# Context rows transposed in one go, modulation columns between two products, one low split moved up, in a two-layer diffusion backbone

## The chip, the cores and the metric

The kernel runs on one core of a Trainium2 chip. The metric is the device time of one execution in microseconds (us); a version's time is the median of its runs. The profile is one execution of the same program, recorded by the hardware profiler.

## The reference

The reference is a small diffusion backbone with two layers, 512 latent tokens `x` and 256 context tokens `ctx`, each of width 1024. Layer 0 is a bidirectional retention mixer, layer 1 a gated spatial mixer (gMLP). Only the start of layer 0 matters here: every row is normalised, scaled and shifted by a vector that comes out of the conditioning `c` (for `x`) or `c_ctx` (for `ctx`), and then multiplied by a wide weight matrix.

```
shift_x, scale_x, gate_x = split(silu(c)     @ ada_w[0] + ada_b[0], 3)
shift_c, scale_c, gate_c = split(silu(c_ctx) @ ada_w[0] + ada_b[0], 3)
hx = rmsnorm(x, norm_g[0])   * (1 + scale_x) + shift_x
hc = rmsnorm(ctx, norm_g[0]) * (1 + scale_c) + shift_c
qx, kx, vx, zx = hx @ w_in;   qc, kc, vc, zc = hc @ w_in
```

`rmsnorm(x, g)` is `x * rsqrt(mean(x*x) + 1e-6) * g`.

## The kernel before

All data are float32. For accuracy each operand of a large product is split into a high part, rounded to the fast matmul type, and a low part, the rest; a product is then three matmuls (low by high, high by low, high by high). The high part is a cast on ScalarE (ACT), the low part a subtraction on VectorE (DVE). The program's names in the profile follow: `hl` is a split weight tile, `raw` the tile as it was loaded, `oA` and `oS` are split pieces of normalised `x`, `hc` is split normalised `ctx`, `xq` and `cq` are the loaded `x` and `ctx`, `pst` is any PSUM bank.

The activations lie transposed, features on the partitions, in K tiles of 128 features. `kb` counts the K tiles from 0 to 7. The first weights to be used are four tiles, B11, B12, B21 and B22: the first index is the half of the features (kb 0 to 3, kb 4 to 7), the second the output columns. `w11` and `w12` in the code are the first two while they are being split in pieces (`cut`, line 692; `Q.begin` gives the tile, `cut(tile, k0, k1)` casts K tiles k0 to k1 of it on ScalarE and returns the low split, which is run where it is called). `Q.upto(n)` splits whole weight tiles until n are done. The weights arrive from HBM through a stream that loads the next tile as soon as a slot is free.

The work at the start, for each K tile, is this:

- `ada0_mm` (line 553) multiplies the conditioning with the modulation weights of one or more K tiles. These are narrow matmuls, 32 columns wide, into a PSUM bank, which ScalarE copies out as `adae`.
- `ada0_cols` (line 569) turns `adae` into columns by transposes on TensorE (PE), and VectorE reduces them and makes the scale `gs` and the shift `sh` of that K tile.
- `come` (line 648) applies them to the rows of that K tile: a scaling on VectorE, the high part on ScalarE, the low part on VectorE.
- `plain` (line 673) multiplies the K tile with the weights. `plain(kb, th, nhs)` does the token half `th` (0 or 1 of `x`, 2 for `ctx`) for the weight tiles in `nhs`, six matmuls for each of the two.

Before `come` can run, the inverse root of each row's mean square is needed. `half_rows(src, g, t)` (line 520) transposes half of the features (`g`) of a block of 256 tokens (`t`; 2 is `ctx`) so that tokens stand on the partitions, in two groups of four transposes with a PSUM bank each; the first group's squares are summed by a Square on ScalarE, the second's by BATCH_NORM_STATS on VectorE. `inverse(t)` (line 531) makes the roots from the two halves, with a Sqrt on ScalarE between small operations on VectorE, and `spread(t)` (line 541) spreads them over the partitions by a product, whose result ScalarE copies to `rs`.

PSUM has eight banks: six for the tag "ps", of which four hold the running sums of the `x` products through this whole stage, and two for the tag "tm", which `ada0_mm`, `ada0_cols` and `spread` share. A tile takes a bank of its tag that is free, or waits until one is.

What is done in which order: TensorE goes in the order of the program text throughout (`pe.kept = True`). ScalarE and VectorE do the same from the first statistics until `hold("c")` behind the loop over kb = 2 to 7 (line 769):

```
    act.kept = dve.kept = True
    ...
    hold("c")
    Q.limit = PROJECTED
    act.kept = dve.kept = False
```

So in this stage an instruction that waits holds up everything behind it on its engine. Behind the loop the two are ordered by the program builder. The loads on SyncE's queue (SP) are issued in the order in which the builder puts them; each of the loads in flight has a semaphore of its own, and the next load is issued when one comes free.

All instructions appear at line 54 in the profile, the helper that records them, so the tiles' names and the times tell them apart.

Of the kernel before, what the change touches and what calls it, by code (L numbers as in the profile page):

```python
# [33 lines left out]
def f32(ap):  # L34
    return ap.bitcast(F32)
# [32 lines left out]
def hybrid_kernel(ctx, tc, xT_d, cT_d, cv_d, sv_d, rows_d, ada0_d, adag_d, w_d, rope_d, dec_d, ws_d, id_d, out_d):  # L68
# [3 lines left out]
    ps = ctx.enter_context(tc.tile_pool(name="ps", bufs=8, space=bass.MemoryType.PSUM))  # L72
# [9 lines left out]
    def st(shape, tag, dt=F32, bufs=1, name=None):  # L82
        return sb.tile(shape, dt, tag=tag, name=name or tag, bufs=bufs)
# [34 lines left out]
    def t2(name, shape=(P, 512), dt=F32):  # L118
        return st(list(shape), "t2", dt, bufs=T2, name=name)

    def pt(shape=(P, 512), tag="ps"):
        return ps.tile(list(shape), F32, tag=tag, name="pst", bufs=6 if tag == "ps" else 2)
# [222 lines left out]
    def features(bank, a, w, fresh, ks=range(4)):  # L345

        for kt in ks:
            if kt == 3 and inside:
                inside.pop(0)()
            r = (a[:, 0, kt, :], a[:, 1, kt, :])  # L350
            for s in range(2):
                o = s * 512 + kt * P
                mm3(bank[:, s * HS:s * HS + HS], (w[:, 0, o:o + P], w[:, 1, o:o + P]), r, fresh and kt == 0 and s == 0, kt == 3)
# [82 lines left out]
    cq = [st([P, 4, HS], f"g{2 + g}", name="cq") for g in range(2)]  # L436
# [80 lines left out]
    mvx = st([P, 3, 2], "mv", name="mvx")  # L517
    sq = [st([P, 2, 2], f"sq{t}", name="sq") for t in range(3)]

    def half_rows(src, g, t):  # L520

        for i in range(2):
            pq = pt()
            for k in range(4):
                pe.transpose(pq[:, k * P:k * P + P], src[:, k, i * P:i * P + P], ident)
            if i == 0:
                act.activation(t2("junk0"), pq, AF.Square, scale=1.0 / 32.0, accum_out=sq[t][:, g, 0:1])
            else:
                dve.bn_stats(bnx[:, t, g, :], pq)

    def inverse(t, then=None):
        s, mv = sq[t], mvx[:, t, :]
        dve.bn_aggr(mv, bnx[:, t, :, :])
        dve.scalar_tensor_tensor(s[:, 1, 1:2], mv[:, 0:1], mv[:, 0:1], mv[:, 1:2], ALU.mult, ALU.add)
        dve.tensor_tensor(s[:, 1, 0:1], s[:, 0, 0:1], s[:, 1, 0:1], ALU.add)
        act.activation(s[:, 1, :], s[:, 1, :], AF.Sqrt, bias=eps, scale=1.0)
        if then:
            then()
        dve.reciprocal(s[:, 1, :], s[:, 1, :])

    def spread(t):

        pr = pt((P, HS), tag="tm")
        for i in range(2):
            mm(pr[:, i * P:i * P + P], sq[t][:, 1, i:i + 1].to_broadcast([P, P]), ident, start=True, stop=True)
        return pr

    def copied(pr, name):
        rs = st([P, HS], name)
        act.copy(rs, pr)  # L550
        return rs

    def ada0_mm(*kbs, then=None):

        n = len(kbs)
        pa = pt((P, HS * n), tag="tm")
        for i, kb in enumerate(kbs):
            rows = ada_w.pop(kb)
            for k in range(KT):
                j = k % 4  # L560
                mm(pa[32 * j:32 * j + 32, i * HS:i * HS + HS], cpad[:, k, :], rows[k // 4][:, j * HS:j * HS + HS],
                   start=(k < 4 and i == 0), stop=(k >= 4), skip_group_check=True)
        if then:
            then()
        e = t2("adae", (P, HS * n))
        act.copy(e, pa)
        return e

    def ada0_cols(k0, e, n=1):
        pq = pt((P, HS * n), tag="tm")  # L570
        for b in range(2 * n):
            pe.transpose(pq[:, b * P:b * P + P], e[:, b * P:b * P + P], ident)
        s = st([P, 2 * n, 2], "ada_s" if n == 1 else "ada_s2", bufs=2, name="ada_s")
        v = pq.rearrange("p (c g r) -> p c r g", c=2 * n, g=4)
        dve.tensor_reduce(s, v[:, :, 0:2, :], axis=AX.X, op=ALU.add)
        ss = s.rearrange("p (n b) r -> p n b r", b=2)
        ks = slice(k0, k0 + n)
        dve.tensor_tensor(gs0[:, ks, :], ss[:, :, 0, :], adab0[:, 1, ks, :], ALU.add)
        dve.tensor_tensor(sh0[:, ks, :], ss[:, :, 1, :], adab0[:, 0, ks, :], ALU.add)
        dve.scalar_tensor_tensor(gs0[:, ks, :], gs0[:, ks, :], 1.0, g0[:, ks, :], ALU.add, ALU.mult)  # L580
# [67 lines left out]
    def come(*what, then=None):  # L648


        made = []
        for kb, th in what:
            g, k = divmod(kb, 4)
            r = th // 2
            if r:
                f, h, l = cq[g][:, k, :], hc[:, 0, kb, :], hc[:, 1, kb, :]
            else:
                name = NAMES[th][g]
                if k == 0:
                    A[name] = st([P, 2, 4, HS], AT_S3.get(name, "o" + name), F32R)  # L660
                f, h, l = xq[th, g][:, k, :], A[name][:, 0, k, :], A[name][:, 1, k, :]
            dve.scalar_tensor_tensor(f, f, gs0[:, kb, r:r + 1], rs[th], ALU.mult, ALU.mult)
            made.append((f, sh0[:, kb, r:r + 1], h, l))
        if then:
            then()
        for f, b, h, l in made:
            act.activation(h, f, AF.Identity, bias=b, scale=1.0)
        for f, b, h, l in made:
            dve.scalar_tensor_tensor(l, f, b, f32(h), ALU.add, ALU.subtract)
# [3 lines left out]
    def plain(kb, th, nhs=range(2), product=None):  # L673

        g = kb // 4
        for nh in nhs:
            if th == 0 and kb % 4 == 0:
                w0[g, nh] = Q.get(ahead=0)
        if th == 2:
            if kb == 0:  # L680
                bank["c"] = pt()
            features(bank["c"], hc[:, :, 4 * g:4 * g + 4, :], w0[g, 0], g == 0, (kb % 4,))
            return
        for nh in nhs:
            if kb == 0:
                bank[th, nh] = pt()
            if product:
                product(bank[th, nh], A[NAMES[th][g]], w0[g, nh], g == 0, kb % 4)
            else:
                features(bank[th, nh], A[NAMES[th][g]], w0[g, nh], g == 0, (kb % 4,))  # L690

    def cut(tile, k0, k1):

        hl, r, done = tile
        at = lambda x: x.rearrange("p (s k n) -> p s k n", s=2, k=4)[:, :, k0:k1, :]
        h, l = at(hl[:, 0, :]), at(hl[:, 1, :])

        def low():
            dve.tensor_tensor(l, at(r), f32(h), ALU.subtract)
            if k1 == 4:  # L700
                done()

        act.copy(h, at(r))
        return low
# [18 lines left out]
    rs[1] = copied(pr, "rs1")  # L723
    w12 = Q.begin()
    plain(0, 1, (0,), features_first)
    ada0_cols(1, es)
    cut(w12, 0, 1)()
    come((1, 0), (1, 1))
    plain(0, 0, (1,), features_first)
    plain(0, 1, (1,), features_first)  # L730
# [24 lines left out]
    def hold(*keys):  # L755

        for key in keys:
            i = len(held)
            if i % 2 == 0:
                two = st([P, 2, 512], f"g{1 + i // 2}", name="held")  # L760
            else:
                two = held[i - 1]
            held[i] = two
            act.copy(two[:, i % 2, :], bank[key])
            plain_done(key if key == "c" else f"{key[0] + 1}{key[1] + 1}", two[:, i % 2, :])
# [3 lines left out]
    for kb in range(2, 8):  # L769
        if kb == 3:  # L770
            Q.upto(3)
        plain(kb, 0)
        if kb in (2, 4, 6):
            ada0_cols(kb + 1, es, 1 if kb == 6 else 2)
        if kb + 1 < 8:
            come((kb + 1, 0), (kb + 1, 1))
        if kb == 4:
            half_rows(cq[1], 1, 2)
            inverse(2)
        if kb in (3, 7):  # L780
            Q.upto({3: 4, 7: 6}[kb])
        plain(kb, 1)
        if kb == 3:
            es = ada0_mm(5, 6)
            half_rows(cq[0], 0, 2)
        if kb == 4:
            es = ada0_mm(7)
        if kb == 2:
            Q.cap = None
            Q.pump()  # L790
        if kb == 4:
            rs[2] = copied(spread(2), "rs2")
        come(*((k, 2) for k in CTX_COME.get(kb, ())))
        if kb == 6:
            Q.upto(5)
        if kb == 7:
            hold((0, 0), (0, 1), (1, 0), (1, 1))
            op("S1")
            dve.tensor_tensor(f22, f21, f22, ALU.add)
            dve.tensor_tensor(shb, sh0[:, 0:4, 0], sh0[:, 4:8, 0], ALU.add)  # L800
            for k in range(4):
                shifted(f22[:, k, :], shb[:, k:k + 1], A["S1"][:, 0, k, :], A["S1"][:, 1, k, :])
        for k in CTX_PLAIN.get(kb, ()):
            plain(k, 2)
# [812 lines left out]
```

## Time and profile before

| | |
|---|---|
| median of 3 runs | 878.79 us (878.61 to 880.75) |
| profiled execution | 878.75 us |
| its span, first to last instruction | 876.7 us |
| TensorE matmul busy | 866.0 us, 99% of the span |
| VectorE busy | 712.2 us, 81% |
| ScalarE busy | 457.2 us, 52% |
| granted TensorE clock, mean | 0.998 |
| moved by DMA | 153.81 MB, mean 175 GB/s |

A row of the timeline gives the start in us from the span's start, the busy time in us, the engine, the line, the operation, `out<-in`, the size and the number of instructions that it merges; in brackets stands the idle time of the engine just before it and what ended that. PE is the matmul, PEld the weight load in front of each matmul, which overlaps with the matmul before; a row of PEld shows best when TensorE went on. A row of a tile of loads gives the issue's time and the time from issue to landing.

### The profile page before, as it was taken

Reading aid. Unit: us, or ns where it says so; the run is one execution under the profiler, and the core shown is the slowest. Engines: PE = TensorE matmul, PEld = TensorE weight load, DVE = VectorE, ACT = ScalarE, POOL = GpSimd, SP = SyncE. Lnnn points to the kernel's source line nnn. Section 1 sums busy time; section 2 is a strip of 40 time slices with the busy share of each in tenths; the row PEclk is TensorE's granted clock in tenths of the full one; section 3 lists DMA queues with packets and bytes.
Section 4 is the critical chain, followed back from the end, with each engine's and each line's share of the span. In section 5 each row is a group of like instructions: output and inputs, shape, how many; then the busy total and the mean of one; then the engine's idle time right before and its main releaser. Section 6 shows DMA issues by size and latency. Waiting matters only on the chain.

```text
span 876.7 us, 16965 instructions
## 1 busy us (share of the span) xinstructions
PE 866.0 (99%) x6890; PEld 826.8 (94%) x6890; DVE 712.2 (81%) x997; ACT 457.2 (52%) x707; POOL 58.3 (7%) x96
## 2 busy tenths in 40 slices
PE   8999999999999999999999999999999999999997
PEld 7799999999999999998989999999999899899986
DVE  4689978699789877878677688999899488688995
ACT  4465744444545435736255548844666546256434
POOL 0001211002101101000000001111000000000110
PEclk9999999999999999999999999999999999999999
DMA  9932967457677458848344511645435135035522
GB/s 349 405 129 97 303 239 267 150 174 241 193 237 243 145 165 328 286 127 272 132 156 158 165 52 70 200 153 196 142 133 180 36 121 192 25 121 168 121 44 102
DMA packets 75774, 153.81 MB, mean 175 GB/s; under 512 B 7728, under 2 KB 34864, under 8 KB 75696
## 3 DMA queue, kind: packets, MB, share of 16 engines
q1 hardware_dynamic: 67392, 128.40, 44.2%
q0 software_dynamic: 7872, 24.12, 8.2%
q8 instruction: 54, 0.88, 0.4%
q10 hardware_dynamic: 432, 0.20, 0.1%
q14 instruction: 24, 0.20, 0.1%
HBM read 128.58 MB, written 24.12 MB: 174 GB/s over the span
## 4 chain that ended last, share of the span: by engine, by line
PE 96%; DVE 1%; DMA 1%; ACT 1%; issue 0%; DVEq 0%; ACTq 0%
PE pst L54 96%; DMA raw<-in_w_dram 1%; DMA xq<-in_xT_dram 0%; DVE o L54 0%; ACT junk L54 0%; DVE xq L54 0%; DVE bnx L54 0%; DVE oA L54 0%; ACT oA L54 0%; ACT fss L54 0%; DVE gs L54 0%; DVE hl L54 0%; DVE sq L54 0%; ACT o L54 0%; DVE ada_s L54 0%
## 5 line engine op out<-in xcount | busy, mean ns | idle before, releaser
L54 DVE TENSOR_TENSOR hl<-raw,hl 128x1024 fp32r<-128x1024 f32 (+2 forms) x197 | 234.8, 1198 | 67.8 <-ACT hl L54 67.5
L54 ACT CAST hl<-raw 128x1024 fp32r<-128x1024 f32 (+2 forms) x197 | 202.8, 1033 | 137.1 <-DVE raw L54 59.3
L54 PE MATMUL pst<-oS,hl 128*128 128x256 f32 x1104 | 133.9, 279 | 0.1
L54 PE MATMUL pst<-hl,oS 128*128 128x256 f32 x1152 | 133.4, 276 | 0.0
L54 PEld LDWEIGHTS pst<-hl,oS 128*128 128x128 f32 x1152 | 131.8, 188 | 1.0 <-ACT snap L54 0.8
L54 PEld LDWEIGHTS pst<-oS,hl 128*128 128x128 f32 x1104 | 129.3, 188 | 1.6 <-PE pst L54 0.8
L54 PE MATMUL pst<-oA,hl 128*128 128x256 f32 x936 | 117.2, 280 | 1.7 <-DVE hl L54 1.2
L54 PEld LDWEIGHTS pst<-oA,hl 128*128 128x128 f32 x936 | 111.2, 188 | 4.5 <-DVE hl L54 1.6
L54 DVE TENSOR_TENSOR raw<-raw 128x1024 f32<-128x1024 f32 x92 | 111.9, 1218 | 0.8
L54 ACT COPY snap<-pst 128x512 f32<-128x512 f32 x92 | 53.6, 584 | 90.5 <-PE pst L54 90.3
L54 PE MATMUL pst<-hl,oA 128*128 128x256 f32 x768 | 91.6, 277 | 0.0
L54 PE MATMUL pst<-og,hl 128*128 128x256 f32 x768 | 91.1, 278 | 0.0
L54 PEld LDWEIGHTS pst<-og,hl 128*128 128x128 f32 x768 | 89.2, 188 | 0.3
L54 PEld LDWEIGHTS pst<-hl,oA 128*128 128x128 f32 x768 | 89.2, 188 | 0.1
L54 PE MATMUL pst<-v,ph 128*128 128x512 f32 x192 | 59.8, 393 | 0.0
L54 PE MATMUL pst<-hl,ya 128*128 128x512 f32 (+1 forms) x246 | 59.1, 386 | 0.0
L54 PEld LDWEIGHTS pst<-hl,ya 128*128 128x128 f32 x246 | 45.3, 188 | 9.5
L54 DVE TENSOR_TENSOR snap<-pst,snap 128x512 f32<-128x512 f32 x69 | 47.2, 684 | 6.2 <-PE pst L54 6.2
L54 PE MATMUL pst<-hl,hc 128*128 128x256 f32 x384 | 46.1, 276 | 0.0
L54 PEld LDWEIGHTS pst<-hl,hc 128*128 128x128 f32 x384 | 44.7, 188 | 0.0
L54 ACT CAST ph<-pf 128x512 fp32r<-128x512 f32 x24 | 14.8, 619 | 54.1 <-DVE pf L54 53.6
L54 PEld LDWEIGHTS pst<-v,ph 128*128 128x128 f32 x192 | 36.1, 188 | 7.3 <-issue 0.2
(181 smaller groups left out, 1022.3 us busy)
## 6 DMA issues: line engine op xcount, KB each, us to landing
raw<-in_w_dram SPq DMA_DIRECT2D x224, 256.0 KB, 4.1
bg<-in_adag_dram SPq DMA_DIRECT2D x32, 512.0 KB, 4.4
ada_w<-in_ada_dram SPq DMA_DIRECT2D x16, 512.0 KB, 9.1
raw<-in_w_dram SPq DMA_DIRECT2D x16, 512.0 KB, 4.3
bg<-in_dec_dram SPq DMA_DIRECT2D x12, 512.0 KB, 4.8
v<-snap POOLq DMA_DIRECT2D x16, 256.0 KB, 5.3
z<-snap POOLq DMA_DIRECT2D x16, 256.0 KB, 5.1
v<-v SPq DMA_DIRECT2D x8, 512.0 KB, 3.8
```

What stands on the lines that cost most here:

```text
L54: made = op(*args, **kw)
```

## The change

Three pieces of work are put elsewhere in the order of the text. None is added or taken out.

1. In the opening, the low split of the first K tile of `w12` stands before `ada0_cols(1, es)`, not behind it.
2. In the loop over kb, `plain(kb, 0)` is cut into its two weight tiles, and `ada0_cols`, where there is one (kb = 2, 4, 6), stands between them, not behind both.
3. The transposes of rows 512 to 1023 of the transposed ctx, that is features 512 to 1023 (`half_rows(cq[1], 1, 2)`), and the roots (`inverse(2)`) stand at the end of kb = 3, directly behind the transposes of the first half, and take their PSUM banks from the tag "tm". Before, they stood in kb = 4, between `come` and the second `plain`. The product that spreads the roots stays at the end of kb = 4.

```diff
-    def half_rows(src, g, t):
+    def half_rows(src, g, t, tag="ps"):
 
         for i in range(2):
-            pq = pt()
+            pq = pt(tag=tag)
...
     plain(0, 1, (0,), features_first)
+    cut(w12, 0, 1)()
     ada0_cols(1, es)
-    cut(w12, 0, 1)()
     come((1, 0), (1, 1))
...
     for kb in range(2, 8):
         if kb == 3:
             Q.upto(3)
-        plain(kb, 0)
+        plain(kb, 0, (0,))
         if kb in (2, 4, 6):
             ada0_cols(kb + 1, es, 1 if kb == 6 else 2)
+        plain(kb, 0, (1,))
         if kb + 1 < 8:
             come((kb + 1, 0), (kb + 1, 1))
-        if kb == 4:
-            half_rows(cq[1], 1, 2)
-            inverse(2)
         if kb in (3, 7):
             Q.upto({3: 4, 7: 6}[kb])
         plain(kb, 1)
         if kb == 3:
             es = ada0_mm(5, 6)
             half_rows(cq[0], 0, 2)
+            half_rows(cq[1], 1, 2, "tm")
+            inverse(2)
         if kb == 4:
             es = ada0_mm(7)
```

## The prediction

> **What bounds the kernel now.** I read the page first, then the chain that ended last in order of time, then the busy times by stretch, and last the timeline of the first 62 us, where every changed line lies.
>
> ```profile
> span 876.7 us, 16965 instructions
> PE 866.0 (99%) x6890; PEld 826.8 (94%) x6890; DVE 712.2 (81%) x997; ACT 457.2 (52%) x707; POOL 58.3 (7%) x96
> 44.08 65.93 PE pst L54 x576
> 60.00:110.00 50.00, 50.00 (x443) 50.00 (x442) 49.28 (x73) 32.60 (x45) 9.63 (x15) 1.00 0.56 183
> ```
>
> TensorE is the bound: it is busy in 99% of the span, and the chain is its own work in long unbroken pieces, one of them from 44.08 to 110. Before it TensorE stands still three times for longer: before 20.10, before 31.90 and before 44.08 (the rows follow, part by part). The changed lines lie at these three stops, and they are all that can be won here. The last row (from 60 to 110 us: stretch, PE, PEld, DVE, ACT, POOL, granted clock, DMA share, GB/s) shows that TensorE is never idle later, but also that VectorE has only 0.7 us to spare there.
>
> The profiled execution took 878.75 us, 2.05 more than its span, and the median shown is 878.79, so a gain read from the trace is taken off 878.75. A measurement of this kernel can tell about 0.3%, 2.64 us, from no change.
>
> **Part 1: low split of the second weight tile before the columns.**
>
> ```profile
> 18.46 0.41 ACT L54 CAST hl<-raw 128x256 fp32r<-128x256 f32 x1
> 18.92 0.30 PEld L54 LDWEIGHTS pst<-oA,hl 128*128 128x128 f32 x2
> 19.11 0.17 DVE L54 TENSOR_REDUCE ada_s<-pst 128x4 f32<-128x16 f32 x1 [0.82 <-PE pst L54]
> 19.62 0.42 DVE L54 TENSOR_TENSOR hl<-raw,hl 128x256 fp32r<-128x256 f32 x1
> 19.96 0.87 DVE L54 SCALAR_TENSOR_TENSOR xq<-xq,gs,rs 128x256 f32<-128x256 f32 x2
> 20.10 0.54 PEld L54 LDWEIGHTS pst<-oA,hl 128*128 128x128 f32 x4 [0.88 <-DVE hl L54]
> 21.45 0.59 PEld L54 LDWEIGHTS pst<-ada_w,cpad 128*32 128x32 f32 x16
> 22.45 0.77 PEld L54 LDWEIGHTS pst<-oA,hl 128*128 128x128 f32 x6 [0.41 <-issue]
> L54 SPq DMA_DIRECT2D ada_w<-in_ada_dram x1: 328/328/328, 12.3 to 12.3; - x1
> DMA to landing us min/median/max: 8.5/8.5/8.5
> ```
>
> The product can do two matmuls with the high half and then needs the low half, which VectorE makes at 19.62, behind four small operations on the modulation columns. Its input, the cast, is there at 18.87, and VectorE is idle until 19.11. Put first, the low half starts at 18.90, ends at 19.32, and TensorE goes on 0.06 later (20.04 to 20.10 now), at 19.38: **0.72 us**. Behind it the reduce starts 0.34 later than the low half (19.62 to 19.96 now), at 19.24, and the next row scaling 0.51 behind that, at 19.75 instead of 19.96, so the columns lose nothing that anyone waits for. What is late next: the modulation product moves from 21.45 to 20.73, and the second half of its weights lands at 12.3 + 8.5 = 20.8, but its ninth matmul is issued about a quarter of its 1.0 us (21.45 to 22.45) in, near 20.97. The 0.72 stands.
>
> **Part 2: columns between the two products of a K tile.**
>
> ```profile
> 27.52 1.48 PEld L54 LDWEIGHTS pst<-oA,hl 128*128 128x128 f32 x12 [0.41 <-issue]
> 27.66 0.59 ACT L54 COPY adae<-pst 128x512 f32<-128x512 f32 x1 [0.73 <-PE pst L54]
> 28.95 0.46 PEld L54 LDWEIGHTS pst<-ident,adae 128*128 128x128 f32 x4
> 29.68 0.19 DVE L54 TENSOR_REDUCE ada_s<-pst 128x8 f32<-128x32 f32 x1 [2.02 <-PE pst L54]
> 30.82 0.51 ACT L54 ACTIVATE oA<-xq,sh 128x256 fp32r<-128x256 f32 x1 [2.57 <-DVE xq L54]
> 31.36 0.48 DVE L54 SCALAR_TENSOR_TENSOR oA<-xq,sh,oA 128x256 fp32r<-128x256 f32 x1 [0.18 <-ACT oA L54]
> 31.38 0.19 PEld L54 LDWEIGHTS pst<-oA,hl 128*128 128x128 f32 x1 [0.56 <-ACT oA L54]
> 31.90 1.36 PEld L54 LDWEIGHTS pst<-oA,hl 128*128 128x128 f32 x11 [0.33 <-DVE oA L54]
> 51.31 0.17 DVE L54 TENSOR_REDUCE ada_s<-pst 128x4 f32<-128x16 f32 x1
> ```
>
> The loop runs for kb = 2 to 7; columns are made at 2, 4 and 6. At kb = 2 the chain from the transposes (28.95) over the reduce (29.68), ScalarE (30.82) and VectorE (31.36 to 31.84) ends the stop at 31.90. Twelve matmuls take 28.95 - 27.52 = 1.43, so six of them, 0.715, leave the path of the transposes. They could start at 27.52 + 0.715 = 28.24 in today's times, but their input is the ScalarE copy that ends at 28.25; with 0.03 to notice it (31.33 to 31.36 between the same two engines' rows), 28.28. The chain is 28.95 - 28.28 = **0.67 us** shorter. The six matmuls themselves are done behind the transposes, where TensorE would else wait 0.56 + 0.33. The stop is longer than what is taken from it, so the whole 0.67 counts; some 0.3 of it stays. At kb = 4 the same move only helps part 3. At kb = 6 the reduce at 51.31 shows no idle time in front of it: VectorE was the late one, and nothing is won or lost.
>
> **Part 3: rows 512 to 1023 of ctx and the roots in kb = 3.**
>
> ```profile
> L54 SPq DMA_DIRECT2D raw<-in_w_dram x1: 328/328/328, 27.0 to 27.0; - x1
> L54 SPq DMA_DIRECT2D cq<-in_cT_dram x1: 328/328/328, 28.3 to 28.3; - x1
> DMA to landing us min/median/max: 7.9/7.9/7.9
> 34.80 1.45 PEld L54 LDWEIGHTS pst<-ada_w,cpad 128*32 128x32 f32 x32
> 35.17 1.03 ACT L54 CAST hl<-raw 128x1024 fp32r<-128x1024 f32 x1
> 36.23 1.23 DVE L54 TENSOR_TENSOR hl<-raw,hl 128x1024 fp32r<-128x1024 f32 x1 [0.45 <-ACT hl L54]
> 36.67 0.86 PEld L54 LDWEIGHTS pst<-ident,cq 128*128 128x128 f32 x8 [0.41 <-issue]
> 36.81 0.58 ACT L54 COPY adae<-pst 128x512 f32<-128x512 f32 x1 [0.61 <-PE pst L54]
> 37.36 0.60 ACT L54 ACTIVATE junk<-pst 128x512 f32<-128x512 f32 x1
> 41.79 0.59 PEld L54 LDWEIGHTS pst<-ada_w,cpad 128*32 128x32 f32 x16
> 42.15 0.69 DVE L54 BATCH_NORM_STATS2 bnx<-pst 128x6 f32<-128x512 f32 x1
> 43.77 0.17 DVE L54 RECIPROCAL sq<-sq 128x2 f32<-128x2 f32 x1 [0.36 <-ACT sq L54]
> 44.05 0.52 PEld L54 LDWEIGHTS pst<-ident,sq 128*128 128x128 f32 x4 [1.67 <-issue]
> 44.49 2.82 PEld L54 LDWEIGHTS pst<-oA,hl 128*128 128x128 f32 x24
> ```
>
> Now the statistics of the second half start at 42.15, the root is ready at 43.94, and the product that spreads it waits until 44.05. The modulation product before it starts at 41.79 and takes 1.0 with its tail (part 1), so 1.26 of this is a stop. No instruction is added: eight transposes, one Square, one BATCH_NORM_STATS and six small ones stand earlier in their queues, and no DMA is moved.
>
> In the new order, with 0.72 + 0.67 = 1.39 taken off: the modulation product starts at 33.41, the first eight transposes at 35.28, the second eight could at 36.10. Their tile lands at 28.3 + 7.9 = 36.2: **0.10 lost**. ScalarE would reach the cast of the fourth weight tile at 35.17 - 1.39 = 33.78, but that tile lands at 27.0 + 7.9 = 34.9, so the cast runs from 34.97. That is the new wait. Behind it on ScalarE stand the copy of the modulation product, from 35.97, and the two Squares, from about 36.5 (0.55 behind the copy, as at 37.36 now) and 37.2 (0.7 for each with the read-out of its sum, an estimate from its 0.60); on VectorE the low half (36.03), two BATCH_NORM_STATS, the roots and only then the reduce of the columns. The second group of four new transposes shares two PSUM buffers ("tm") with that copy, which ends at 36.55; TensorE is there at 36.2 + 0.43 = 36.63 (half of the 0.86), so it does not wait. The eight end at 37.06, and the columns' transposes at kb = 4 come up at 37.06 + 0.715 = 37.77, and need the buffer that the second Square frees near 37.9: **0.14 lost**. The root then takes the 1.79 from 42.15 to 43.94, counted from about 37.8, and is ready near 39.6. The spreading product comes up only at 41.6. What is late next is the first half of kb = 5: its reduce stands behind the roots, near 39.55, and by the row distances of part 2 (29.68 to 31.84) its low half is ready near 41.7, against a product at 42.06: 0.3 to spare. So the stop of 1.26 goes and 0.24 comes: **1.02 us**. From the spreading product on, ScalarE, VectorE and TensorE all follow it, so the shift is handed on whole, and the long piece from 44.08 starts earlier by the sum.
>
> Sum: 0.72 + 0.67 + 1.02 = 2.41 us, 878.75 - 2.41 = **876.3 us**, 0.27% less. Not in the trace are the landings under the new order: as they stand they cost 0.24; 0.3 earlier they cost nothing, 0.5 later they cost about 0.5 more. I take them as they stand, since the queue is full in this stretch (413 to 418 GB/s below) and its order is unchanged. If all of the last two stops went (0.89 and 1.26, beside the 0.72), the gain would be 2.87; that is the ceiling.
>
> ```profile
> 27.50:31.00 3.50, 3.50 (x32) 3.29 (x28) 1.41 (x7) 0.77 (x2) 0.00 (x0) 1.00 1.04 418
> 31.00:34.80 3.80, 3.30 (x25) 2.96 (x24) 3.08 (x6) 2.11 (x5) 0.00 (x0) 1.00 1.03 413
> 41.80:44.50 2.70, 1.48 (x21) 0.86 (x21) 1.70 (x7) 1.04 (x4) 0.00 (x0) 1.00 1.09 368
> ```
>
> The Trainium skill, page "DMA: Bandwidth & Descriptors", section "Where 436 GB/s comes from", puts the ceiling of the ports at 435 GB/s and HBM's share of one core at about 358. The trace's 413 to 418 is past the second figure and 4% short of the first; at the ceiling both landings would come over 1 us earlier (an estimate) and the sum would be 2.65 instead of 2.41.
>
> **The rivals.** *A, the landings do not bite*, and perhaps what I leave of the stop in part 2 goes too: gain 2.65 to 2.87, 876.1 to 875.9. For it: a tile's landing needs only 0.3 us. Against: a full queue.
>
> *B, the roots' chain is late.* If the columns at kb = 4 get the PSUM buffer that the second half's BATCH_NORM_STATS frees, on VectorE behind a low half of 1.23, they wait until 38.5 instead of 37.9, and with landings 0.5 later they lose 1.1 in all: gain 1.3 to 1.8, 877.5 to 876.9. Against: ScalarE's part of the work is shorter by the rows above.
>
> *C, the clock falls.* The transposes and the narrow modulation product now stand in one piece of 33.41 to 37.06. If such work did not hold the clock, 3.5 us of full TensorE work (the row from 27.50) at half speed would cost 3.5: 879.8; two such pieces 883.3. It decides from 2.4 us lost. The Trainium skill, page "TensorE: Matmul & The Clock Gate", section "Part 4: PE-mode transpose", says that a transpose does not count as busy for the clock. Against it by the rows: the stretch with TensorE busy 1.48 of 2.70 us has a granted clock of 1.00, and so has every other.
>
> *D, slower by a changed order later on.* ScalarE and VectorE are held to the order of the text only up to the end of this loop; behind it the builder orders them by readiness. From 60 to 110 VectorE is busy 49.28 of 50. If one low split of 1.23 is put ahead of one that TensorE waits for, TensorE loses up to 1.23. Two such cancel the gain (878.8), five make 882.5. For it: the little room on VectorE. Against: all three engines are shifted alike, so nothing there becomes ready in another order.
>
> **How the numbers follow.** Forecast 0.52, with 2.1 to 2.9 us gained, 0.22 of it over 2.64; A 0.24; B 0.10; C 0.05, of which 0.03 beyond 0.3% slower; D 0.09, of which 0.08. Faster by over 0.3%: 0.22 + 0.24 = 0.46. Within: 0.30 + 0.10 + 0.02 + 0.01 = 0.43. Slower: 0.11. The range runs from A's far end, 875.9, to B's, 877.5, each with 0.4 to 0.5 for the spread of runs (the three shown differ by 0.2 and 2.1): 875.5 to 878.0. C and D are outside.
>
> **What would show it.** Right: TensorE goes on near 19.4 (part 1), starts kb = 3 near 30.5 (part 2), the reciprocal of the ctx roots ends near 39.6, the spreading product waits for nothing, and the long piece of the chain starts near 41.7. The cast of the fourth weight tile should sit behind a DMA, and the columns at kb = 4 behind a Square. Wrong: a wait of TensorE of over 0.5 us at kb = 4 or 5 (B), a granted clock under 1.00 before 50 us (C), new idle time of TensorE after 60 us (D).

## The result, and the profile after

The changed kernel takes 877.73 us in the median of 22 runs (876.75 to 879.20), the kernel before, run beside it, 878.79 (878.29 to 880.75). The ratio is 0.9984, with a 95% interval of 0.9978 to 0.9991: 1.4 us faster, between 0.8 and 1.9 (the two medians alone differ by 1.06). That lies inside the 0.3% that the prediction called no change, to which it gave a chance of 0.43 against 0.46 for more. It lies inside its range, but it is little more than half of the 2.41 us forecast.

The profiled execution of the kernel after took 879.01 us, with a span of 876.9, so it shows no gain at all. Its page, the lines of the span and of the busy times:

```profile
span 876.9 us, 16967 instructions
PE 868.4 (99%) x6890; PEld 829.7 (95%) x6890; DVE 713.0 (81%) x997; ACT 457.9 (52%) x707; POOL 58.4 (7%) x96
```

TensorE is busy 2.4 us longer than before (866.0) with the same 6890 matmuls. Two things make up most of that, and only one of them belongs to the change. The first is in the opening. The timeline of the kernel before, then that of the kernel after (start, busy time, engine, line, operation, tiles, count):

```profile
7.74 0.91 PEld L54 LDWEIGHTS pst<-ident,xq 128*128 128x128 f32 x8
16.64 0.59 PEld L54 LDWEIGHTS pst<-ada_w,cpad 128*32 128x32 f32 x16
25.66 0.81 PEld L54 LDWEIGHTS pst<-ada_w,cpad 128*32 128x32 f32 x20
```

```profile
8.75 1.66 PEld L54 LDWEIGHTS pst<-ident,xq 128*128 128x128 f32 x8
18.39 0.59 PEld L54 LDWEIGHTS pst<-ada_w,cpad 128*32 128x32 f32 x16
```

The same eight transposes take 0.91 in one execution and 1.66 in the other. No line of the change has run by then, yet everything in the trace of after is 1.75 us later when the modulation product of kb = 1 starts (18.39 against 16.64). It is TensorE's clock, which in this one execution became fast some 3.5 us later: in the traces' own record the full clock is granted from 6.80 us on before and from 10.28 on after. (The clock column of the view by stretch does not tell the two apart. It reads 1.00 from 7 to 10.2 us of after as well, where the transposes are slow, because the record begins only at 10.28.) So the two spans must not simply be subtracted. A second execution of the kernel after, below, has the early clock. Behind that start, the timeline of after reads:

```profile
20.51 0.42 DVE L54 TENSOR_TENSOR hl<-raw,hl 128x256 fp32r<-128x256 f32 x1 [0.47 <-ACT hl L54]
20.55 0.99 PEld L54 LDWEIGHTS pst<-oA,hl 128*128 128x128 f32 x6
22.38 0.59 PEld L54 LDWEIGHTS pst<-ada_w,cpad 128*32 128x32 f32 x16
29.19 0.42 PEld L54 LDWEIGHTS pst<-ident,adae 128*128 128x128 f32 x4
29.89 0.19 DVE L54 TENSOR_REDUCE ada_s<-pst 128x8 f32<-128x32 f32 x1 [1.35 <-PE pst L54]
32.11 1.32 PEld L54 LDWEIGHTS pst<-oA,hl 128*128 128x128 f32 x11 [0.23 <-DVE oA L54]
34.92 1.45 PEld L54 LDWEIGHTS pst<-ada_w,cpad 128*32 128x32 f32 x32
36.78 1.73 PEld L54 LDWEIGHTS pst<-ident,cq 128*128 128x128 f32 x16 [0.41 <-issue]
40.42 0.17 DVE L54 RECIPROCAL sq<-sq 128x2 f32<-128x2 f32 x1 [0.36 <-ACT sq L54]
41.88 0.59 PEld L54 LDWEIGHTS pst<-ada_w,cpad 128*32 128x32 f32 x16
42.88 0.52 PEld L54 LDWEIGHTS pst<-ident,sq 128*128 128x128 f32 x4 [0.41 <-DVE oA L54]
43.32 2.81 PEld L54 LDWEIGHTS pst<-oA,hl 128*128 128x128 f32 x24
```

All three edits do what they were to do. The six matmuls at 20.55 run through, where there was a stop of 0.88. Before kb = 3 a stop of 0.23 is left. The sixteen transposes of ctx stand in one piece at 36.78, and the first product of kb = 5 follows the modulation product of kb = 7 by 1.44 us (41.88 to 43.32), where it was 2.70 (41.79 to 44.49). From the modulation product of kb = 1 to the first product of kb = 5 the kernel after takes 24.93 us and the kernel before 27.85: 2.92 less, even more than the forecast ceiling of 2.87.

That gain is then partly given back. The stretch from 186 to 222 us, in the busy times by stretch, before and then after (the number in brackets counts the matmuls):

```profile
186.00:222.00 36.00, 36.00 (x320) 36.00 (x320) 33.77 (x39) 16.25 (x21) 5.04 (x8) 1.00 0.73 237
```

```profile
186.00:222.00 36.00, 36.00 (x308) 36.00 (x307) 32.94 (x37) 15.22 (x20) 5.06 (x8) 1.00 0.73 239
```

TensorE is busy all the time at a granted clock of 1.00 in both. But it gets 320 matmuls done before and 308 after: one each 112.5 ns, then each 116.9 ns. Two marks in the timeline, one product on each side of that stretch, before and then after:

```profile
157.11 2.89 PEld L54 LDWEIGHTS pst<-oA,hl 128*128 128x128 f32 x24
225.25 0.14 PEld L54 LDWEIGHTS pst<-ada_a,ones 128*32 128x32 f32 x4
```

```profile
155.94 2.89 PEld L54 LDWEIGHTS pst<-oA,hl 128*128 128x128 f32 x24
225.03 0.14 PEld L54 LDWEIGHTS pst<-ada_a,ones 128*32 128x32 f32 x4
```

The same matmuls on the same operands take 68.14 us before and 69.09 after: 0.95 us lost far behind the last changed line, with no wait to be seen.

### The profile page after: what moved, and what is told of

Same layout as the page of the kernel before. It is cut to its first block, busy times and chain, and to the rows that moved or that the text cites. A ratio compares the mean times of both kernels' runs of the same rounds, so it can differ in the third digit from the quotient of the medians.

```text
span 876.9 us, 16967 instructions
## 1 busy us (share of the span) xinstructions
PE 868.4 (99%) x6890; PEld 829.7 (95%) x6890; DVE 713.0 (81%) x997; ACT 457.9 (52%) x707; POOL 58.4 (7%) x96
## 4 chain that ended last, share of the span: by engine, by line
PE 97%; DVE 1%; DMA 1%; ACT 0%; issue 0%; ACTq 0%; DVEq 0%
PE pst L54 97%; DMA ident<-in_id_dram 1%; DVE o L54 0%; ACT junk L54 0%; DVE bnx L54 0%; DVE xq L54 0%; ACT fss L54 0%; DVE sq L54 0%; ACT o L54 0%; DVE fss L54 0%; ACT oS L54 0%; DVE oA L54 0%; ACTq L455 0%; DVE mvx L54 0%; DVE hl L54 0%
```

## The experiments

In all of them each kernel ran 11 times beside the kernel before, and the ratio is to those runs of the kernel before, not to the 878.79 of the first row. One table holds what they share. "kb 1-2" is the time from the start of the modulation product of kb = 1 to that of kb = 2, "2-3" on to that of kb = 3, "3-5" on to that of kb = 5, "5-7" on to that of kb = 7, and "7-P" on to the first product of kb = 5. "Stage" is their sum, and "marks" the time between the two marks just shown (157.11 to 225.25 in the kernel before). All are differences of two starts in the timeline of the profiled execution.

| kernel | median, us | ratio (95%) | kb 1-2 | 2-3 | 3-5 | 5-7 | 7-P | stage | marks |
|---|---|---|---|---|---|---|---|---|---|
| before | 878.79 | | 4.81 | 4.21 | 9.14 | 6.99 | 2.70 | 27.85 | 68.14 |
| after | 877.73 | 0.9984 (0.9978-0.9991) | 3.99 | 4.17 | 8.37 | 6.96 | 1.44 | 24.93 | 69.09 |
| e1 before, again | 879.37 | 1.0000 (0.9992-1.0009) | 4.81 | 4.21 | 9.06 | 6.98 | 2.70 | 27.76 | 68.14 |
| e2 after, again | 877.62 | 0.9983 (0.9974-0.9992) | 3.95 | 5.02 | 8.47 | 7.05 | 1.44 | 25.93 | 69.10 |
| e3 part 3 alone | 878.31 | 0.9997 (0.9988-1.0006) | 4.81 | 4.22 | 9.05 | 6.99 | 1.44 | 26.51 | 69.09 |
| e4 parts 1 and 2 | 878.01 | 0.9989 (0.9980-0.9998) | 3.95 | 4.44 | 8.39 | 7.19 | 2.10 | 26.07 | 68.14 |
| f1 part 1 alone | 878.47 | 0.9998 (0.9989-1.0007) | 3.95 | 4.66 | 9.06 | 6.98 | 2.69 | 27.34 | 68.14 |
| f2 no landing at kb = 2 | 877.77 | 0.9984 (0.9975-0.9993) | 3.98 | 4.19 | 9.02 | 7.21 | 1.45 | 25.85 | 69.10 |
| f3 two more warm-ups | 877.77 | 0.9988 (0.9979-0.9997) | 3.95 | 4.64 | 8.39 | 7.15 | 1.45 | 25.58 | 69.10 |
| f4 old PSUM tag | 879.24 | 1.0005 (0.9996-1.0013) | 3.95 | 4.99 | 8.39 | 8.43 | 1.44 | 27.20 | 69.10 |
| g1 after, slots back | 877.94 | 0.9986 (0.9977-0.9995) | 3.95 | 4.54 | 8.38 | 7.39 | 1.44 | 25.70 | 69.09 |
| g2 before, slots changed | 878.98 | 1.0000 (0.9991-1.0009) | 4.80 | 4.21 | 9.05 | 6.99 | 2.69 | 27.74 | 68.14 |
| g3 g1 with two more warm-ups | 877.76 | 0.9988 (0.9979-0.9996) | 5.06 | 4.22 | 8.38 | 6.96 | 1.44 | 26.06 | 69.09 |
| h1 one more wait | 877.48 | 0.9983 (0.9974-0.9992) | 3.95 | 4.21 | 8.81 | 7.53 | 1.44 | 25.94 | 69.09 |

### Both kernels again, and the parts alone

e1 and e2 are the two kernels unchanged; e3 takes only the third edit, e4 the first two, f1 the first.

```diff
# e3
-            pq = pt()
+            pq = pt(tag=tag)
...
-        if kb == 4:
-            half_rows(cq[1], 1, 2)
-            inverse(2)
...
             half_rows(cq[0], 0, 2)
+            half_rows(cq[1], 1, 2, "tm")
+            inverse(2)
# e4 (f1: the first two lines only)
+    cut(w12, 0, 1)()
     ada0_cols(1, es)
-    cut(w12, 0, 1)()
...
-        plain(kb, 0)
+        plain(kb, 0, (0,))
...
+        plain(kb, 0, (1,))
```

> The kernel before once more, unchanged, to see how far two profiles of one program differ. Stage time means from the weight load of the kb = 1 modulation product to that of the first product of kb = 5: 27.85 us in the profile before, 24.93 in the profile after. Theory A (the stage keeps its gain, the rest is chance: the moment at which TensorE's fast clock begins, and stretches in which the same matmuls come 118 instead of 113 ns apart): stage time 27.7 to 28.0, but the start of the fast clock and the matmuls at the slower spacing (1074 in the profile before) differ between the two profiles by hundreds. Theory B (the change lengthens those stretches and so gives gain back): again about 1074 of them, and the same total.

> The changed kernel once more, unchanged. Both theories: stage time 24.9 where the fast clock begins late, up to 25.4 where it begins early, since then two landings are met. Theory A: number of matmuls at the slower spacing other than 1376, by chance, and a gain in the median of 1 to 2.6 us. Theory B: 1376 within 100, and a gain of 1.0 to 1.6 us.

> Only the ctx rows and the roots are moved, with their PSUM banks from the other tag; the two other edits are undone. By the rows of before the stop of 1.26 us goes and no landing is met, since TensorE comes 1.4 later than with all three: stage time 26.6 (27.85 less 1.26), time 1.2 to 1.3 under before. If the landings or the shared banks were what costs, it would stay over 27.0.

> Only the low split and the columns are moved; the ctx rows and roots are where they were. By the prediction's first two terms 0.72 + 0.67: stage time 26.4 to 26.5, time 1.4 under before, and the stop in front of the spreading product stays at 1.2 to 1.3. If the third stop grew by what the first two lose, because something fixed in time ends it, stage time would stay at 27.8.

> Only the low split of the second weight tile is moved. The prediction gave it 0.72 us and 0.15 us to spare before the second half of the modulation weights of kb = 2 lands. In the repeated profiles that half landed at 20.92 to 21.92, not at 20.83. Theory A (this landing takes back part of the term): the weight load of that product's second half waits for the DMA by 0.3 to 1.1 us, and the time from the product of kb = 1 to the first product of kb = 2 (16.64 to 22.45, 5.81, in the profile before; 4.99 without a landing) is 5.2 to 5.8. Rival (the split itself gains less, because VectorE is late): no DMA wait there, and TensorE still idle behind a VectorE split. Time 0.1 to 0.7 under before.

e1 and e2 bear out a part of each theory. In the two traces of the kernel before, 1044 and 1236 weight loads start 116 to 119 ns behind the one in front of them; in the two of the kernel after it is 1324 and 1169 (the 1074 and 1376 of the expectations are by another count). So the total moves by 192 and by 155 from one execution of the same program to the next, as theory A has it, but the time between the marks does not move, as theory B has it. The stage of e3 came out as expected. That of e4 is 0.3 to 0.4 shorter than expected, since a part of the third stop went with the first two edits. f1 met the wait that its theory A expected, 0.77 us.

The timeline of e2, with the early clock:

```profile
18.48 0.97 PEld L54 LDWEIGHTS pst<-oA,hl 128*128 128x128 f32 x6
20.27 0.16 PEld L54 LDWEIGHTS pst<-ada_w,cpad 128*32 128x32 f32 x8
21.51 0.16 PEld L54 LDWEIGHTS pst<-ada_w,cpad 128*32 128x32 f32 x8 [1.08 <-DMA ada_w<-in_ada_dram]
33.76 1.45 PEld L54 LDWEIGHTS pst<-ada_w,cpad 128*32 128x32 f32 x32
35.29 1.05 ACT L54 CAST hl<-raw 128x1024 fp32r<-128x1024 f32 x1 [1.07 <-DMA raw<-in_w_dram]
38.12 0.46 PEld L54 LDWEIGHTS pst<-ident,adae 128*128 128x128 f32 x4
39.74 0.17 DVE L54 RECIPROCAL sq<-sq 128x2 f32<-128x2 f32 x1 [0.36 <-ACT sq L54]
40.81 0.59 PEld L54 LDWEIGHTS pst<-ada_w,cpad 128*32 128x32 f32 x16
41.81 0.52 PEld L54 LDWEIGHTS pst<-ident,sq 128*128 128x128 f32 x4 [0.41 <-issue]
42.25 2.36 PEld L54 LDWEIGHTS pst<-oA,hl 128*128 128x128 f32 x20
```

The third row is the point: the ninth matmul of the modulation product of kb = 2 waits 1.08 us for the second half of its weights. In the table it is the column "2-3": 5.02 against 4.21. e4 and f1 show the same wait, shorter. In the trace of after, which started 1.75 us later, the weights were there (they landed at 21.15, the product begins at 22.38, and "2-3" is 4.17). That makes 0.85 of the microsecond by which its stage is shorter than that of e2. The weights do not come later because TensorE comes earlier: their landing, issue and time to landing added, is at 20.83 in the trace of before, at 21.92 and 21.34 in e1 and e3, which do not have the first edit, and at 21.47, 20.92 and 21.01 in e2, e4 and f1, which do. By these figures the landings do not follow TensorE's time.

Column by column the parts are then clear. Part 1 takes 0.82 to 0.86 off "kb 1-2" in all kernels that have it but g3, and loses between nothing (h1, where the weights landed at 19.93) and 0.8 of it at the landing in "2-3". In g3 nothing is won: "kb 1-2" is 5.06 against 4.81. There the low split came first as well, but its input, the cast, waited for the weight tile itself:

```profile
19.16 0.40 ACT L54 CAST hl<-raw 128x256 fp32r<-128x256 f32 x1 [1.01 <-DMA raw<-in_w_dram]
```

That tile lands at 17.22 to 18.38 us in the other thirteen traces (18.38 in that of before) and at 19.08 in g3. Part 2 takes 0.67 off "3-5" in e2 (8.47 against the 9.14 of before) and up to 0.77 in the others that have it without a new landing. The other four traces without part 2 show 9.05 or 9.06; against them it is 0.58 or 0.59 in e2 and 0.66 to 0.69 in the others. Part 3 takes 1.26 off "7-P" in every kernel that has it. In e4, which keeps the second half of ctx at kb = 4, 0.6 of that stop goes as well, and 0.2 is paid in "5-7".

The times agree only roughly with this. e3 gains 1.3 us in the stage and shows no gain at all in its ratio; f1's 0.5 is not to be told from nothing; e4's 1.8 appear as 1.0 (0.2 to 1.8). The last column says why for e3 and e2: with part 3 the time between the marks is 0.95 longer than in all kernels without it. For e2 that leaves 1.9 - 0.95 = 0.95 us, and its ratio says 1.5 (0.7 to 2.3). By the same working e4, which loses nothing between the marks, should beat e2 by 0.8. In the traces it does, by 0.7 (spans of 874.6 and 875.3 us), but in the medians it does not. The execution of e4 that was profiled took 876.70 us. It and one of 876.71 are the fastest of the eleven, and the other nine took 877.61 to 878.70. Whether those nine had another spacing is not on record, since only one execution of each kernel was profiled. So the 0.95 is shown for the profiled executions, and not for all.

### Is the landing at kb = 2 what keeps the gain down?

f2 reads the first half of the weights of kb = 2 twice, so that the modulation of that K tile is another one and the second half need not have landed.

```diff
-  cpad[:, k, :], rows[k // 4][:, j * HS:j * HS + HS],
+  cpad[:, k, :], rows[0 if kb == 2 else k // 4][:, j * HS:j * HS + HS],
```

> All three edits, but the modulation product of kb = 2 reads the first half of its weights twice, so that it does not need the second half, which is still loaded; the modulation of that K tile is therefore another one. Theory A: without the wait of 1.08 us on this landing the stage takes 25.0 to 25.4 us (25.93 with it, where the fast clock began as early), the cast of the fourth weight tile and the ctx tile still wait for their landings, and the median is 0.5 to 0.9 us under the changed kernel's 877.6. Rival (the landing is hidden, since the later landings are met anyway): stage 25.8 to 26.0 and the same time as the changed kernel.

The wait of "2-3" is gone (4.19), but the stage is 25.85 against 25.93 and the median the same, as the rival has it. The reason stands in the timeline of f2:

```profile
24.62 1.02 PEld L54 LDWEIGHTS pst<-ada_w,cpad 128*32 128x32 f32 x24
26.47 0.16 PEld L54 LDWEIGHTS pst<-ada_w,cpad 128*32 128x32 f32 x8 [0.82 <-DMA ada_w<-in_ada_dram]
```

Now the product of kb = 3 and 4 waits, for the next load in the same queue. "3-5" is 9.02 where it is 8.4 in the others. A landing removed uncovers the next one. h1 shows the same without any such edit: there the weights of kb = 2 happened to land early, "2-3" is 4.21, and the next load is met:

```profile
26.15 0.16 PEld L54 LDWEIGHTS pst<-ada_w,cpad 128*32 128x32 f32 x8 [0.63 <-DMA ada_w<-in_ada_dram]
```

So in the early part of this opening TensorE can be moved earlier only by what the landings leave.

### Two more warm-up matmuls

```diff
-N_WARM = 10
+N_WARM = 12
```

> All three edits, with 12 in place of 10 filling matmuls in the opening. They fill the 0.5 to 0.65 us in which TensorE waits for the first transposes. Theory A on the clock (the fast clock begins at the end of a fixed interval in which TensorE was busy enough; the pause in front of the transposes sometimes makes it miss one, and then the opening takes 1.8 us longer): the late begin, at 10 us, no longer comes, the slowest runs are less than 1.5 us above the fastest (2.4 for the changed kernel over 22 runs), the median falls by 0.1 to 0.5. Rival (the begin of the clock is pure chance): the spread stays at 2 us or more. If the two matmuls delay the transposes instead: 0.2 to 0.4 slower.

The median does not move (877.77). The 11 runs of f3 lie within 0.9 us (877.29 to 878.21), where the 22 of the kernel after span 2.45. That shows nothing of the warm-up, though: with 10 filling matmuls the 11 runs of e1, f2, g1 and g2 lie within 0.84 to 1.10 us as well, and the full clock begins at 6.21 us in the trace of f3, later than in seven of the twelve traces with 10. Whether two more would prevent the late start stays open.

### Is the other PSUM tag needed?

```diff
-            half_rows(cq[1], 1, 2, "tm")
+            half_rows(cq[1], 1, 2)
```

> All three edits, but the second half of the ctx rows takes its PSUM banks from the tag of the first half, which has two free. By the changed kernel's rows its first four transposes wait for the Square of the first half (ends near 37.3 in the repeated profile) and the next four for its BATCH_NORM_STATS (near 38.2), where with the other tag they start at 36.5 and 37.0: stage 0.9 to 1.3 us longer than 25.93 with an early clock, time 0.6 to 1.3 us over the changed kernel. If banks do not matter: the same stage.

The timeline of f4:

```profile
36.08 0.85 PEld L54 LDWEIGHTS pst<-ident,cq 128*128 128x128 f32 x8 [0.41 <-issue]
38.05 0.42 PEld L54 LDWEIGHTS pst<-ident,cq 128*128 128x128 f32 x4 [1.12 <-ACT junk L54]
38.85 0.42 PEld L54 LDWEIGHTS pst<-ident,cq 128*128 128x128 f32 x4 [0.38 <-DVE bnx L54]
```

With four of the six "ps" banks held by the running sums, the second half waits for the Square (1.12) and for BATCH_NORM_STATS (0.38) of the first. "5-7" grows to 8.43, 1.38 over e2, and the kernel takes 879.24 us. The tag is worth 1.3 us in the stage (27.20 against 25.93), as expected, and 1.5 in the median, a little more than the 0.6 to 1.3 expected.

### What spaces the matmuls out behind the loop?

Without an exception, the nine kernels in the table that have part 3 take 69.09 or 69.10 us between the marks and the five without it 68.14. The matmuls between, their operands' places and their PSUM banks are the same in both sorts by the program, and so, between e3 and the kernel before, is the order of the instructions of ScalarE and VectorE behind the loop. I looked for something that part 3 moves as a side effect. The first find was a pair of the 2 KB tiles (`t2`): the tiles of the second Square and of the fifth and sixth modulation product become free in the other order, and two of the 11 slots change places in everything that follows. g1 turns that back in the kernel after, g2 does it in the kernel before, each by one small GpSimd copy that keeps the other tile in use longer; g3 is g1 with N_WARM 12.

```diff
# g1 (and g3)
+                junk[t, g] = t2("junk0")
-                act.activation(t2("junk0"), pq, AF.Square, ...
+                act.activation(junk[t, g], pq, AF.Square, ...
...
             rs[2] = copied(spread(2), "rs2")
+            nc.gpsimd.tensor_copy(junk[2, 1][:, 0:1], rs[2][:, 0:1])
# g2
-            es = ada0_mm(5, 6)
+            es = es56 = ada0_mm(5, 6)
...
             rs[2] = copied(spread(2), "rs2")
+            nc.gpsimd.tensor_copy(es56[:, 0:1], rs[2][:, 0:1])
```

> The kernel after, with one small instruction more: GpSimd copies one column into the junk tile of the second ctx Square, behind the copy of the spread roots at kb=4. It keeps that junk tile in use longer than the tile of the fifth and sixth modulation products, so that the small tiles of 512 columns (11 slots) are given out in the order of the kernel before: slots 7 and 9 change places in all that follows the loop. Theory (the microsecond given back behind the loop comes with the two slots): the stretch of matmuls at 118 ns from about 182 to 224 us is gone and the short one at about 157 to 184 us is back, the time from the first product of kb=5 to the end is 832.2 to 833.0 us instead of 833.0 to 833.8, and the median is about 876.7, 1.0 under the kernel after (ratio about 0.997). Rival (the stretch comes with the earlier start or with the order in which the roots of ctx are made, wherever the small tiles lie): the stretch at 182 to 224 us stays, 833.0 to 833.8 and a median of 877.7 (ratio 0.998).

> The kernel before, with the same small GpSimd instruction, but into the tile of the fifth and sixth modulation products: nothing of the change is made, only slots 7 and 9 of the small tiles change places behind the loop, as in the kernel after. Theory (slots): the stretch of matmuls at 118 ns from about 182 to 224 us appears, the time from the first product of kb=5 to the end is 833.0 to 833.8 instead of 832.2 to 833.0, and the median is about 880.0, 1.0 over the kernel before (ratio about 1.001). Rival (earlier start or order of the roots): no difference from the kernel before, 832.2 to 833.0 and a median of 878.9 to 879.1.

> The kernel after with the small GpSimd instruction of the run before last (slots as in the kernel before) and with N_WARM 12 instead of 10, which narrowed the spread of its runs. Theory (slots): as that run, time from the first product of kb=5 to the end 832.2 to 833.0, median about 876.7, with a spread of about 1 us over its runs. Rival: 833.0 to 833.8, median 877.8.

Busy times by stretch, g1 and then g2:

```profile
186.00:222.00 36.00, 36.00 (x308) 36.00 (x308) 32.91 (x38) 15.07 (x19) 5.05 (x8) 1.00 0.72 233
```

```profile
186.00:222.00 36.00, 36.00 (x320) 36.00 (x320) 33.69 (x38) 16.01 (x21) 5.05 (x8) 1.00 0.75 236
```

The theory falls, on both sides: with the slots of the kernel before, g1 still gets only 308 matmuls done, and g2, with those of the kernel after, 320. g3 is as g1. The second find was TensorE's own program: part 3 needs one instruction less that only waits (71 instead of 72), so all that follows stands one place earlier in the stream. h1 adds such a wait early in the loop, by a second identity tile:

```diff
+    ident2 = st([P, P], "rs2", name="ident2")
+    nc.gpsimd.tensor_copy(ident2, ident)
...
-  e[:, b * P:b * P + P], ident)
+  e[:, b * P:b * P + P], ident2 if k0 == 3 else ident)
```

> The kernel after, with a copy of the identity tile (made by GpSimd at the start) for the transposes of the modulation columns at kb=2. These then wait for two engines instead of one, and TensorE's program has one more instruction that only waits: 72 of them, as in the kernel before, where the kernel after has 71. Everything behind the loop then stands at the same number in TensorE's program as in the kernel before. Theory (the spacing of the matmuls behind a stop depends on where they stand in TensorE's stream of instructions): the stretch at 118 ns from about 182 to 224 us is gone and that of about 157 to 184 us is back, the time from the first product of kb=5 to the end is 832.2 to 833.0 us, with the stretch at 549 to 572 us deciding between the two, and the median is about 876.7 (ratio about 0.997), 1.0 below the kernel after. Rival (it comes with the earlier start or with the roots made at kb=3): the stretch at 182 to 224 us stays, 833.0 to 833.8, median 877.7. Both expect the start of the loop as in the kernel after, within 0.3 us.

```profile
186.00:222.00 36.00, 36.00 (x308) 36.00 (x307) 32.91 (x38) 15.06 (x19) 5.05 (x8) 1.00 0.73 238
```

308 again: this falls too. What is left is what the timeline shows of where the spacing turns, before and then e2:

```profile
167.27 1.83 PEld L54 LDWEIGHTS pst<-oS,hl 128*128 128x128 f32 x15
184.22 1.91 PEld L54 LDWEIGHTS pst<-hl,oA 128*128 128x128 f32 x16
```

```profile
165.06 2.80 PEld L54 LDWEIGHTS pst<-oS,hl 128*128 128x128 f32 x24
181.39 2.89 PEld L54 LDWEIGHTS pst<-hl,oA 128*128 128x128 f32 x24
```

Between these two rows lie 144 matmuls: 16.95 us before (117.7 ns each), 16.33 in e2 (113.4). Behind the second row it is the other way round (the 320 and 308 of the stretch). The two kernels leave a short stop for transposes, just ahead of the first row, with different spacing, and both change to the other spacing where the weight tile passes from the moving to the stationary operand. Read so, the spacing is a state that TensorE keeps, that turns over at stops and changes of operands, and that in the kernels with part 3 is the other way round from one such stop on. That is a reading of these rows and not tested by itself. Since the second stretch is more than twice as long as the first, the kernel before has the better side of it. Which property of part 3 does it stays open. The slots, the place in the stream and the order of the other engines behind the loop are excluded by g1, g2, h1 and e3. So is the tag: f4 has the old one and still takes 69.10. So is an earlier start alone: e4, without part 3, starts the first product of kb = 5 at 42.39 us and takes 68.14, while f4, with it, starts it later, at 44.08.

No version that was run is faster than the kernel after by more than the intervals. The one with the least in its trace is e4 (876.70 us in its profiled execution, the lowest of its 11 runs), but its median is 878.01.

## Why the prediction was right, and where not

**What bounds the kernel:** right. The gain and the losses are all TensorE's, and the opening is the only place where a wait was taken away.

**Part 1:** the term was nearly right (0.82 to 0.86 in "kb 1-2", forecast 0.72), but it stood on a landing that the working does not name: the cast at 18.46 came 0.08 behind the landing of its tile at 18.38. That tile mostly landed earlier, which made the term larger, and in g3 it landed at 19.08 and took the whole term. The sentence behind the term was wrong. "The 0.72 stands" rested on 0.15 us between a landing at 20.8 and the ninth matmul at 20.97, both from one execution. Over the fourteen traces the landing comes at 19.93 to 22.04, and the start of the stage lies at 16.18 to 16.88 where the clock was early. In e2 0.81 was lost there. A margin of 0.15 was no margin; it should have been a term with a range. It is rival A turned round: the landings bit in a place where the forecast had none.

**Part 2:** right in size (0.67 forecast; 0.58 to 0.77 measured, depending on the trace without part 2 that it is set against) and in what stays of the stop: 0.23 in the row at 32.11, some 0.3 forecast.

**Part 3:** right. The stop of 1.26 went whole. The cast of the fourth weight tile waits for a DMA, as forecast, until 35.29 (34.97 forecast, the landing 0.3 later). The reciprocal starts at 39.74 and ends at 39.91 (39.6), the spreading product comes up at 41.81 with nothing to wait for (41.6). The wait of 0.14 for the second Square is not in e2: the ctx tile landed at 36.47, TensorE came late enough, and the columns' transposes follow their matmuls at 38.12. In all "5-7" lost 0.06 instead of 0.24, and up to 0.54 in h1, where TensorE reached kb = 5 earlier against the same landing of the ctx tile (36.49).

**The sum:** 2.41 was forecast with the landings as they stood; e2 has 1.9, and the trace of after, for which the landings came in time, 2.92. The ceiling of 2.87 was a good figure for a kernel without landings. The two spans of before and e2 differ by 1.40 (876.7 and 875.3): 0.32 less before the stage, which is not the change's, 1.92 less in the stage, 0.02 more up to the first mark, 0.96 more between the marks, and 0.14 less behind them.

**"From the spreading product on the shift is handed on whole":** this is the step that failed. It holds as far as the first mark: from the first product of kb = 5 to it take 112.62 us before (44.49 to 157.11) and 112.64 in e2 (42.25 to 154.89). VectorE, with 0.7 us to spare, did no harm there. (In h1 it is 113.11; 0.23 of the excess is a stop of TensorE before 100.39, the only one between 60 us and the first mark that the timelines of the fourteen traces show.) Then 0.95 is lost to the spacing, for which the sum had no term. The argument looked at waits and at order, and a slower repetition of the same instruction is neither.

**The rivals:** A holds only in an execution that starts late. B did not happen. C did not: the sixteen transposes run at 1.73 us, the same 108 ns each as before (0.86 for eight). It is this duration that decides: the granted clock that the prediction named as its sign reads 1.00 even where the opening was slow. That agrees with the trace of before and speaks against what the Trainium skill, page "TensorE: Matmul & The Clock Gate", section "Part 4: PE-mode transpose", would make of it: here a piece of 3.5 us of transposes and narrow products did not lower the clock. D named the right place, behind the loop, with the wrong mechanism: in e3 ScalarE and VectorE keep the order of the kernel before there, and 0.95 is lost all the same.

So the number was within range partly by luck. Against the sum, 0.95 was lost where nothing was expected and 0.5 at landings. The measured 877.73 lies beyond the far end of B, 877.5, and inside the range only by the 0.4 to 0.5 that was added for the spread of runs.

## What to carry to other kernels

When work is moved earlier in an opening that loads at a full queue, compare it with the range of landings over several executions, not with one: the next landing is always close behind. Compare two traces only from a point where both have the same clock, and add up stage by stage, since a span can hide a gain of 2 us. A gain behind which thousands of matmuls follow should be checked by counting matmuls per stretch, because busy time and waits do not show a slower repetition.

## What the runs showed of the hardware

**Two spacings of the same matmul.** Pairs of weight load and matmul with 256 columns repeat each 112.5 to 113.4 ns or each 117 to 118 ns at a granted clock of 1.00, for tens of microseconds. In the rows shown, the spacing turns at a stop or at a change of the operands. The time between the marks is the same to 0.01 us in every kernel of a sort, and the twelve kernels e1 to h1 were profiled on four different chips. One further stretch, from 550 to 570 us, has either state in both sorts: 177 matmuls in the trace of before, 173 in that of after, 172 in that of e1, worth some half a microsecond (4 or 5 matmuls). The Trainium skill, page "TensorE: Matmul & The Clock Gate", section "Wait — 56ns, not 53.3ns?", gives, for matmuls back to back, the columns at 2.4 GHz and 2.5 ns more, which is 109.2 ns here (an estimate). Here a weight load stands in front of each matmul, and both measured spacings are above that, by 3 to 4 and by about 8 ns.

**The start of the fast clock.** The eight transposes that took 0.91 and 1.66 us show that two executions can come to full speed about 3.5 us apart with no changed line run by then, which cost 1.75 us. The record of the full clock lasts 866.99 us in eight of the fourteen traces, 870.40 in five and 863.57 in that of after: steps of 3.41 us. In both of the first two sorts the stage starts within 16.18 to 16.88. The same page, section "What's actually happening", says that the activity of TensorE is judged in windows of about 3.4 us that run freely; the traces agree with steps of one window, and that of after with a start that misses one.

**Landings.** The same load of 512 KB, the second half of the weights of kb = 2, landed between 19.93 and 22.04 us in the fourteen traces, with the same order of loads.
